# Staging the next layer's parameters and the sample state right behind the pooling, with a longer ring of input tiles, in a four-layer trunk

## The chip, the cores and the metric

The kernel runs on all 8 cores of one Trainium2 chip, each core with one prompt and 16 sample rows. The time is device microseconds of the slowest core. A program on 8 cores has a second, slower state in some executions, in which the cores of a die show a lower granted clock; fast runs are compared with fast runs here. Faster, same, slower are drawn at 2%. In the profiles PE is TensorE (the matrix engine, which also does the transposes), DVE is VectorE, ACT is ScalarE, POOL is the Pool engine (GpSimd) and SP is SyncE. A slab is one block of weights, a head one of the eight heads of the spatial step.

## The reference, cut to what matters

```python
for l in range(4):                       # for the prompt and for the sample rows
    z = rmsnorm(x, g_pre_mix) @ w_in      # columns a | u | v | gate_a | gate_b
    ya, new_buf = pool_mixer(a, buf, ...) # trailing means over 2..16 rows; the sample rows start from a state
    v = layernorm(gelu(v));  s = tril(W_s[h]) @ v + b_s[h]     # per head, chunks of 128 rows
    m = sigmoid(ga) * (ya @ w_ba) + sigmoid(gb) * ((gelu(u) * s) @ w_bb)
    x = x + rmsnorm(m @ w_out, ...)
    x = x + rmsnorm(relu(rmsnorm(x) @ w_up)**2 @ w_down, ...)
```

## The kernel before: the parts that matter

A core works through three blocks of rows (768, 768, and 512 plus the 128 sample rows), four layers each, in 128-row tiles: 6, 6 and 5 of them. The weights come as 30 slabs a layer (2 MB of f32 read, 1 MB of bf16 written) into 8 places.

A scheduler emits every instruction with the semaphore waits that its declared reads and writes need. A write waits for the last writer and for all readers of the name. Two things run through the Pool engine in one order: the issue of all slab loads and of the casting parameter loads, and the small steps of each norm, `(var + eps)` and `** -0.5`.

```python
def pool_dma(writes, out, in_, cost):
    key = ("g", nxt("g", 4))
    S.op("pool", [], writes, lambda e: e.dma_start(out=out, in_=in_), semkey=key, inc=16, ...)

def stage_params(l, par, ae):             # ae: the four names of the pooling buffer, which the parameters overlay
    pool_dma(["raw16"] + ae, raw16, w_spT[l]..., 1.5)
    pool_dma(["bb16"] + ae, bb16, ln_b[l:l + 1, :]..., 1.5)
    pool_dma(["wpg"], wpg[:, :, :], w_pg[l]..., 0.8)
    S.dma([], ["bsb"] + ae, bsb..., b_sp[l:l + 1, :]...)
```

The second load names `ae` too, so it waits until the first has landed.

The order of one layer, cut:

```python
head: clear or copy the first 15 columns of the pooling buffer; sample block: load the state, copy it in
for n in (0, 1):                          # two sub-blocks of tiles
    a_stage; start pooling (VectorE); u_stage; v_stage of each tile; start its LayerNorm chain
pool_proj(1)
for j in range(8):
    gate, branch A for j;  if j == 0: flush the LayerNorm chains;  spatial(j, 0); spatial(j, 1)
branch B, output projection, up-projection (first half)
CH.drain(); stage_params(next layer)      # no norm is in flight here
up-projection (second half), prep of the staged parameters between its slabs
down-projection; norm of each tile; start the next layer's norm, or store the tile and load the next block's
```

Of the kernel before, what the change touches and what calls it, by code (L numbers as in the profile page):

```python
# [170 lines left out]
def build():  # L171
# [35 lines left out]
    with es:  # L207
# [3 lines left out]
        def sb(name, shape, dt):  # L211
            return es.enter_context(nc.sbuf_tensor(name, shape, dt))

        x = sb("x", [128, 7, 1024], F32)
        hTb = sb("hTb", [128, 8 * TMAX], BF16)
        R2 = sb("R2", [128, 32 * TMAX], BF16)
        R1 = sb("R1", [128, 4 * AW], F32)
# [18 lines left out]
        invcnt = sb("invcnt", [128, 4, 15], F32)  # L236
        atail = sb("atail", [128, DEPTH, 4, 15], F32)
        t3 = [sb(f"t3_{i}", [128, 16], F32) for i in range(2)]
        spst = sb("spst", [128, 4, 16, 15], F32)
        stt = sb("stt", [128, 6, 8], F32)  # L240
        vstats = sb("vstats", [128, 6, 2, 6], F32)
        vmv = sb("vmv", [128, 6, 2], F32)
# [79 lines left out]
            return (b0[:, 0:512].bitcast(BF16).rearrange("p (h t) -> p h t", h=8), b0[:, 512:1024].bitcast(BF16),  # L322
                    b1.rearrange("p (h t) -> p h t", h=8))

        def stage_params(l, par, ae):
            raw16, bb16, bsb = par
            pool_dma(["raw16"] + ae, raw16, w_spT[l].rearrange("p (h t) -> p h t", h=8), 1.5)
            pool_dma(["bb16"] + ae, bb16, ln_b[l:l + 1, :].broadcast_to([128, 1024]), 1.5)
            pool_dma(["wpg"], wpg[:, :, :], w_pg[l].rearrange("p (g d) -> p g d", g=4), 0.8)
            S.dma([], ["bsb"] + ae, bsb.rearrange("p h t -> p (h t)"), b_sp[l:l + 1, :].broadcast_to([128, 1024]))  # L330

        def load_g(key, buf, src, l):
            S.dma([], [key], buf[:], src[l:l + 1, :].broadcast_to([128, 1024]))
# [40 lines left out]
        def group(parts, N, M=128):  # L374
            b = bank()
            total = sum(len(p[1]) for p in parts)
            at = 0
            for reads, mms in parts:
                pace()
                CH.pump()  # L380

                def emit(e, mms=mms, at=at):
                    for q, (lh, rh) in enumerate(mms):
                        r = e.matmul(ps[b][:, 0:N], lhsT=lh, rhs=rh, start=(at + q == 0), stop=(at + q == total - 1))  # L384
                    return r
                S.op("pe", reads, [("ps", b)], emit, cost=mm_us(len(mms), N))
                at += len(mms)
            CH.pump(False)
            return b

# [96 lines left out]
            return (BLOCKS[bi][1] + (128 if BLOCKS[bi][2] else 0)) // 128  # L487

        def xslot(bi, i):
            return (6 * bi + i) % 7  # L490

        def load_x(bi, i, after=[]):
            k = xslot(bi, i)
# [12 lines left out]
        for i in range(3):  # L506
            launch(i, lambda i=i: start_norm(i, xslot(0, i), views(768)["hT"]))
            need_hT([i])
            if i < 2:
                load_next()  # L510
        pool_dma(["trilT"], trilT[:], c_tril, 0.3)
        stage_params(0, par0, [])
        for i in range(3, 6):
            load_x(0, i, [("hT", i - 3)])
            launch(i, lambda i=i: start_norm(i, xslot(0, i), views(768)["hT"]))
# [6 lines left out]
        for bi, (p0, npr, samp) in enumerate(BLOCKS):  # L522
# [7 lines left out]
            if samp:  # L530
                gslot = xslot(bi, NT)
                gb32 = x[:, gslot, :]
                spare = R2[:, 32 * T:32 * T + 4096].bitcast(F32)
                bb32, vsamp = spare[:, 0:1024], spare[:, 1024:2048]

            for l in range(DEPTH):
# [3 lines left out]
                nsamp = has_next and BLOCKS[nbi][2]  # L540


                head = [("aext", g) for g in range(4)] + ["raw16", "bb16", "bsb"] + [("og0", i) for i in range(6)]
                if bi == 0:
                    S.op("dve", [], head,
                         lambda e: e.memset(aext[:, :, 0:15], 0.0), cost=0.15)
# [1 line left out]
                    S.op("dve", [("atail", l)], head,  # L548
                         lambda e: e.tensor_copy(out=aext[:, :, 0:15], in_=atail[:, l, :, :]), cost=0.15)
                if samp:  # L550
                    S.dma([], ["spst"], spst[:].rearrange("p g q r -> p (g q r)"), sp_in[l])
                    sx = aext[:, :, SBASE:SBASE + 368].rearrange("p g (q r) -> p g q r", r=23)
                    for g in range(4):
                        S.op("dve", ["spst"], [("aext", g)],
                             lambda e, g=g: e.tensor_copy(out=sx[:, g, :, 0:15], in_=spst[:, g, :, :]), cost=0.4)
                    R2tail = [] if l else [("fT", j, n) for j in range(32) for n in range(2)]
                    S.dma([], ["gb32", ("x", gslot)], gb32, ln_g[l:l + 1, :].broadcast_to([128, 1024]))
                    S.dma([], ["bb32"] + R2tail, bb32, ln_b[l:l + 1, :].broadcast_to([128, 1024]))
# [24 lines left out]
                def a_outputs():  # L583
                    ae = [("aext", g) for g in range(4)]
                    if bi < len(BLOCKS) - 1:
                        S.op("dve", ae, [("atail", l)],
                             lambda e: e.tensor_copy(out=atail[:, l, :, :], in_=aext[:, :, npr:npr + 15]), cost=0.15)
                    if samp:
                        S.op("dve", ae, ["atail_o"],
                             lambda e: e.tensor_copy(out=atail[:, l, :, :], in_=aext[:, :, npr:npr + 15]), cost=0.15)  # L590
                        S.dma(["atail_o"], [("spp", l)], spp[l], atail[:, l, :, :].rearrange("p g w -> p (g w)"))
                        for g in range(4):
                            S.op("dve", ae, ["spst"],
                                 lambda e, g=g: e.tensor_copy(out=spst[:, g, :, :], in_=sx[:, g, :, 8:23]), cost=0.4)
                        S.dma(["spst"], [("sps", l)], sps[l], spst[:].rearrange("p g q r -> p (g q r)"))

                def pool_chain(g, seg, ta, tb, tk, t3x, t3k):
                    kind, c0, L, n = seg
# [118 lines left out]

                for n, (n0, N) in enumerate(subs):
                    need_hT(stiles[n])
                    if n == 1:  # L720
                        load_g("gpre", gpre, g_pre_f, l)
                        load_g("gpost", gpost, g_pm, l)
                    a_stage(n, n0, N)
                    if n == 1:
                        a_outputs()
                        CH.flush(pooled)
                        release(bi, l, SL_A)
                    segs = []
                    pe_ = min(n0 + N, npr)
                    if pe_ > n0:  # L730
                        segs.append(("p", n0, pe_ - n0, n))
                    if samp and n == 1:
                        segs.append(("s", 0, 8, 1))
                    last_pooled = CH.start(pooling(segs))
                    u_stage(n, n0, N)
                    if n == 1:
                        pool_proj(0, *subs[0])
                    pooled = last_pooled
                    for i in stiles[n]:
                        v_stage(i)  # L740
                    if n == 0 and bi == 0 and l == 0:
                        for ph in range(3):
                            prep(samp, ph, par0)
                for q in (SL_U, SL_U + 1, SL_V, SL_V + 1):
                    release(bi, l, q)
                CH.flush(pooled)
                pool_proj(1, *subs[1])


                def gate(j, n, first, step):  # L750
# [50 lines left out]
                for j in range(8):  # L801
# [2 lines left out]
                        branch_a(j, n, q)  # L804
                    if j == 3:
                        release(bi, l, SL_GA)
                    if j == 0:
                        for c in ln:
                            CH.flush(c)
                    for n in range(2):  # L810
                        spatial(j, n)
                    if samp and j == 2:
                        S.op("dve", vk + ["gb32"], vk,
                             lambda e: e.tensor_tensor(out=vsamp, in0=vsamp, in1=gb32, op=ALU.mult), cost=1.2)
# [110 lines left out]
                load_g("gpost", gpost, g_pf, l)  # L925
                if last and has_next:
                    load_x(nbi, 0)
                if has_next:
                    stage_params(nl, parR, [("aext", g) for g in range(4)])
                    load_g("gpre", gpre, g_pre_m, nl)  # L930
                for s8 in range(4, 8):
                    for jj in range(4):
# [7 lines left out]
                for i in range(NT):  # L940
                    n = 0 if i < 3 else 1
                    parts = []
                    for q in range(4):
                        kw, sv = slab_kn(bi, l, SL_DN + q, 8)
                        parts.append(([kw] + [("fT", 8 * q + k, n) for k in range(8)],
                                      [(fT[:, 8 * q + k, i * 128:(i + 1) * 128], sv[:, k, :]) for k in range(8)]))
                    b = group(parts, 512)
                    if i == NT - 1:
                        for q in range(4):
                            release(bi, l, SL_DN + q)  # L950
                    jq = nxt("junk", 2)
                    S.op("act", [], [("ps", b), ("st", i, 0), ("junk", jq)],
                         lambda e: e.activation(out=junk[jq][:, 0:512], in_=ps[b][:, :], func=AF.Square, scale=1.0 / 32.0,  # L953
# [8 lines left out]
                def ffn_chain(i, b, q, bi=bi, last=last, has_next=has_next, nbi=nbi, nV=nV):  # L962
# [16 lines left out]
                    if not last:  # L979
                        launch(i, lambda: start_norm(i, xk, nV["hT"]))  # L980
                    else:
                        S.dma([("x", xk)], [("y", bi, i)], x_dst(bi, i), x[:, xk, :], lat=6.0)
                        if has_next and i + 1 < ntiles(nbi):
                            yield S.ready(("y", bi, i)), False
                            load_x(nbi, i + 1)
                            launch(i + 1, lambda: start_norm(i + 1, xslot(nbi, i + 1), nV["hT"]))

                if last and has_next:
                    launch(0, lambda: start_norm(0, xslot(nbi, 0), nV["hT"]))

                ffn = {}
                for i in range(NT):
                    n = 0 if i < 3 else 1
                    parts = []
                    for q in range(4):
                        kw, sv = slab_kn(bi, l, SL_DN + 4 + q, 8)
                        parts.append(([kw] + [("fT", 8 * q + k, n) for k in range(8)],
                                      [(fT[:, 8 * q + k, i * 128:(i + 1) * 128], sv[:, k, :]) for k in range(8)]))
                    b = group(parts, 512)
                    if i >= 2:  # L1000
                        CH.flush(ffn[i - 2])
                    ffn[i] = CH.start(ffn_chain(i, b, i % 2))
                for q in range(4):
                    release(bi, l, SL_DN + 4 + q)
                for i in range(NT):
                    CH.flush(ffn[i])
            if bi == len(BLOCKS) - 1:
# [94 lines left out]
```

## Time and profile before

| | before |
|---|---|
| fast runs | 3795.09, 3794.92 us (its other two, 3874.82 and 4460.84 us, were slow) |
| span of the 8 cores in the profiled run | 3772.0 to 3795.0 us |
| granted TensorE clock | 0.990 to 0.993 |
| TensorE busy | 3667.3 us, 97% |

A table of waits reads: engine, line and what it writes, then what ended the wait, then the total in us, the number of waits and the longest.

### The profile page before, as it was taken

Reading aid. Unit: us, or ns where it says so; the run is one execution under the profiler, and the core shown is the slowest. Engines: PE = TensorE matmul, PEld = TensorE weight load, DVE = VectorE, ACT = ScalarE, POOL = GpSimd, SP = SyncE. Lnnn points to the kernel's source line nnn. Section 1 sums busy time; section 2 is a strip of 40 time slices with the busy share of each in tenths; the row PEclk is TensorE's granted clock in tenths of the full one; section 3 lists DMA queues with packets and bytes.
Section 4 is the critical chain, followed back from the end, with each engine's and each line's share of the span. In section 5 each row is a group of like instructions: output and inputs, shape, how many; then the busy total and the mean of one; then the engine's idle time right before and its main releaser. Section 6 shows DMA issues by size and latency. Waiting matters only on the chain.

```text
span 3795.0 us, 63764 instructions; the slowest of 8 cores (3772.0 to 3795.0 us)
## 1 busy us (share of the span) xinstructions
PE 3667.3 (97%) x22021; PEld 2105.6 (55%) x22208; DVE 1764.7 (47%) x3385; ACT 1160.6 (31%) x2528; POOL 527.6 (14%) x1219
## 2 busy tenths in 40 slices
PE   6999999999999999999999999998899999999999
PEld 3554555555455455555545555553565665664664
DVE  3642652563455256246426525642552752752752
ACT  2331332323233133323313323241332331331331
POOL 1111110111101011011111101111011111111110
PEclk9999999999999999999999999999899999999999
DMA  8484766658467675755756666595677777777773
GB/s 165 81 149 76 124 107 103 112 98 147 78 112 117 116 152 96 135 98 92 127 97 112 103 111 111 92 157 125 130 119 143 137 124 143 137 124 141 140 121 86
DMA packets 75194, 449.32 MB, mean 118 GB/s; under 512 B 9472, under 2 KB 11136, under 8 KB 28800
## 3 DMA queue, kind: packets, MB, share of 16 engines
q0 software_dynamic: 57456, 385.48, 61.9%
q1 hardware_dynamic: 17424, 59.76, 5.1%
q8 instruction: 185, 3.03, 0.3%
q14 instruction: 129, 1.06, 0.1%
HBM read 817.55 MB, written 13.10 MB: 219 GB/s over the span
## 4 chain that ended last, share of the span: by engine, by line
PE 92%; DMA 5%; issue 1%; DVE 1%; ACT 0%; POOL 0%; DVEq 0%; SPq 0%; ACTq 0%; POOLq 0%
PE ps L384 84%; PE ps L883 6%; DMA R<-w_spT 2%; PE ps L439 2%; DMA R<-b_sp 1%; DMA R<-ln_b 1%; PE ps L778 1%; DMA x<-xp 1%; DMA spst<-sp 1%; ACT R L393 0%; DVE ps L837 0%; DVE hTb L445 0%; PE ps L364 0%; DVE x L976 0%; DVE R L685 0%
## 5 line engine op out<-in xcount | busy, mean ns | idle before, releaser
L384 PE MATMUL ps<-hTb,wslot 128*128 128x384 bf16 (+1 forms) x11520 | 1868.1, 319 | 18.3 <-DVE Cm L369 9.4
L384 PEld LDWEIGHTS ps<-hTb,wslot 128*128 128x128 bf16 x11520 | 1125.1, 98 | 668.9 <-issue 41.1
L384 PE MATMUL ps<-wslot,R 128*128 128x512 bf16 x4254 | 938.9, 379 | 5.3 <-issue 0.2
L393 ACT ACTIVATE R<-ps 128x384 bf16<-128x384 f32 (+5 forms) x1208 | 576.8, 482 | 958.7 <-PE ps L384 913.8
L384 PEld LDWEIGHTS ps<-wslot,R 128*128 128x128 bf16 x4352 | 424.5, 98 | 503.7 <-issue 0.2
L901 DVE TENSOR_TENSOR R<-R 128x384 bf16<-128x384 bf16 (+1 forms) x768 | 263.0, 346 | 558.6 <-ACT R L393 556.5
L384 PE MATMUL ps<-R,wslot 128*128 128x384 bf16 (+1 forms) x2304 | 414.1, 318 | 0.6
L306 POOL DMA_DIRECT2D wslot<-wslab x360 | 201.5, 563 | 971.5 <-PE ps L384 479.2
L393 ACT ACTIVATE sg<-ps 128x384 bf16<-128x384 f32 (+1 forms) x384 | 179.8, 471 | 495.9 <-PE ps L384 262.0
L384 PEld LDWEIGHTS ps<-R,wslot 128*128 128x128 bf16 x2304 | 225.2, 98 | 129.8 <-issue 3.4
L431 DVE SCALAR_TENSOR_TENSOR hst<-x,stt,gpre 128x1024 bf16<-128x1024 f32 x136 | 174.4, 1283 | 164.1 <-POOL stt L404 161.3
L956 DVE TENSOR_TENSOR R<-ps,gpost 128x512 f32<-128x512 f32 x68 | 47.1, 692 | 432.3 <-ACT junk L953 432.3
L883 PE MATMUL ps<-wslot,R 128*128 128x512 bf16 x1024 | 234.7, 379 | 3.4
L384 PE MATMUL ps<-wslot,hTb 128*128 128x512 bf16 x1063 | 233.7, 379 | 1.3
L422 ACT ACTIVATE hst<-x 128x1024 bf16<-128x1024 f32 x136 | 143.5, 1055 | 193.8 <-DVE x L976 122.5
L384 PEld LDWEIGHTS ps<-wslot,hTb 128*128 128x128 bf16 x1088 | 106.4, 98 | 125.6
L953 ACT ACTIVATE junk<-ps 128x512 bf16<-128x512 f32 x68 | 40.6, 597 | 427.1 <-PE ps L384 427.1
L883 PEld LDWEIGHTS ps<-wslot,R 128*128 128x128 bf16 x1088 | 105.6, 98 | 116.4
L404 POOL TENSOR_TENSOR stt<-stt,mhalf 128x1 f32<-128x1 f32 x272 | 163.4, 601 | 40.1 <-POOL stt L426 0.6
L837 DVE TENSOR_TENSOR ps<-ps,sg 128x384 f32<-128x384 f32 (+1 forms) x192 | 104.1, 542 | 128.5 <-PE ps L384 127.1
L854 ACT ACTIVATE junk<-ps 128x512 bf16<-128x512 f32 x136 | 81.2, 597 | 270.2 <-PE ps L883 247.1
L706 DVE BATCH_NORM_STATS2 vstats<-R 128x6 f32<-128x512 bf16 x128 | 88.9, 694 | 155.5 <-ACT R L393 155.5
(73 smaller groups left out, 1817.2 us busy)
## 6 DMA issues: line engine op xcount, KB each, us to landing
wslot<-wslab POOLq DMA_DIRECT2D x360, 1024.0 KB, 16.4
x<-xp SPq DMA_DIRECT2D x16, 512.0 KB, 6.9
yp<-x SPq DMA_DIRECT2D x16, 512.0 KB, 9.8
gpre<-g_pre_m SPq DMA_DIRECT2D x12, 512.0 KB, 21.1
R<-b_sp SPq DMA_DIRECT2D x12, 512.0 KB, 12.9
gpre<-g_pre_f SPq DMA_DIRECT2D x12, 512.0 KB, 15.0
gpost<-g_pm SPq DMA_DIRECT2D x12, 512.0 KB, 21.2
gpost<-g_pf SPq DMA_DIRECT2D x12, 512.0 KB, 5.1
```

The source lines that it names most:

```text
L306: lambda e: e.dma_start(out=wslot[k][:, :], in_=wslab[l, s]), semkey=("w", k), inc=16, cost=5.7, lat=2.0)
L384: r = e.matmul(ps[b][:, 0:N], lhsT=lh, rhs=rh, start=(at + q == 0), stop=(at + q == total - 1))
L393: lambda e: e.activation(out=out, in_=in_, func=func, **kw), cost=act_us(N))
L404: lambda e: e.tensor_tensor(out=col, in0=ss, in1=mhalf[:, 0:n], op=ALU.pow))
L422: lambda e: e.activation(out=hst[q][:, :], in_=x[:, k, :], func=AF.Square, scale=1.0 / 32.0, accum_out=stt[:, i, 4:5]), cost=1.2)
L431: lambda e: e.scalar_tensor_tensor(out=hst[q][:, :], in0=x[:, k, :], scalar=stt[:, i, 5:6], in1=gpre[:, :], op0=ALU.mult, op1=ALU.mult), c ...
L439: r = e.transpose(out=pT16[:, c * 128:(c + 1) * 128], in_=hst[q][:, c * 128:(c + 1) * 128], identity=ident16[:])
L706: lambda e: e.bn_stats(out=vstats[:, i, half, :], in_=B3[:, i, cs]), cost=0.69)
L837: lambda e: e.tensor_tensor(out=ps[b][:, 0:N], in0=ps[b][:, 0:N], in1=sgring[q][:, 0:N], op=ALU.mult), cost=dve_us(N))
L854: lambda e, b=b, ci=ci: e.activation(out=junk[jq][:, 0:512], in_=ps[b][:, :], func=AF.Square, scale=1.0 / 32.0, accum_out=stt[:, i, ci:ci ...
L883: r = e.matmul(ps[b][:, :], lhsT=B2[:, k, i * 128:(i + 1) * 128], rhs=wo[:, k, :], start=(k == 0), stop=(k == 7))
L901: lambda e: e.tensor_tensor(out=fT[:, j, n0:n0 + N], in0=fT[:, j, n0:n0 + N], in1=fT[:, j, n0:n0 + N], op=ALU.mult), cost=dve_us(N, 2))
```

## The change

Its intent: take the waits at the block boundaries, at the layer ends of the sample block and at the start out of TensorE's way. Cut to its core (lines left out or gathered; where the source has an edit in several places it stands once):

```diff
-        x = sb("x", [128, 7, 1024], F32)
+        x = sb("x", [128, 8, 1024], F32)          # the state now lies in a free place of this ring
 # start
-            if i < 2:
-                load_next()                        # slabs 2, 3 between the first norms
+        load_next(); load_next()                   # after the third norm
-        stage_params(0, par0, [])
+        stage_params(0, par0, [], [("hT", 0)])     # b_sp waits for the first norm
 # head of a layer
-    head = [...aext...] + ["raw16", "bb16", "bsb"] + [...]
+    head = [...aext...] + [...];  if bi or l: head += ["raw16", "bb16", "bsb"]
-    S.dma([], ["spst"], ..., sp_in[l]);  copy spst into aext      # sample block
+    if l == 0: S.dma([], ["spst", ("x", sslot)], ..., sp_in[l])
 # sub-block n == 1
+    if n == 1 and samp: copy spst into aext
 # behind the pooling
     CH.flush(pooled)
     pool_proj(1, *subs[1])
+    if has_next:
+        stage_params(nl, parR, [("aext", g) for g in range(4)])
+    if samp and not last:
+        S.dma([], ["spst"], ..., sp_in[l + 1])
 # gates
-    if j == 0: flush the LayerNorm chains
-    for n in range(2): spatial(j, n)
+    if j == 1: flush the LayerNorm chains
+    for h in ((), (0,), (1,), (2,), (3,), (4, 5), (6,), (7,))[j]:
+        for n in range(2): spatial(h, n)
 # up-projection
-    stage_params(nl, parR, [("aext", g) for g in range(4)])
 # down-projection: each slab is released after its own part of the last tile, not all four at the end
 # next block: tiles 0 and 1 loaded ahead, tile i + 2 (not i + 1) after the store of tile i
```

More of the change, by code (lines that the diff above doesn't have):

```diff
@@ L238, in build @@
         t3 = [sb(f"t3_{i}", [128, 16], F32) for i in range(2)]
-        spst = sb("spst", [128, 4, 16, 15], F32)
         stt = sb("stt", [128, 6, 8], F32)
@@ L323, in par_views_of, with stage_params @@
                     b1.rearrange("p (h t) -> p h t", h=8))
-        def stage_params(l, par, ae):
+        def stage_params(l, par, ae, after=[]):
             raw16, bb16, bsb = par
@@ L329, in stage_params @@
             pool_dma(["wpg"], wpg[:, :, :], w_pg[l].rearrange("p (g d) -> p g d", g=4), 0.8)
-            S.dma([], ["bsb"] + ae, bsb.rearrange("p h t -> p (h t)"), b_sp[l:l + 1, :].broadcast_to([128, 1024]))
+            S.dma(after, ["bsb"] + ae, bsb.rearrange("p h t -> p (h t)"), b_sp[l:l + 1, :].broadcast_to([128, 1024]))
         def load_g(key, buf, src, l):
@@ L377, in group @@
             at = 0
-            for reads, mms in parts:
+            for part in parts:
+                reads, mms = part[:2]
                 pace()
@@ L387, in group @@
                 at += len(mms)
+                if len(part) > 2:
+                    part[2]()
             CH.pump(False)
@@ L489, in xslot @@
         def xslot(bi, i):
-            return (6 * bi + i) % 7
+            return (6 * bi + i) % 8
         def load_x(bi, i, after=[]):
@@ L508, in build @@
             need_hT([i])
-            if i < 2:
-                load_next()
+        load_next()
+        load_next()
         pool_dma(["trilT"], trilT[:], c_tril, 0.3)
-        stage_params(0, par0, [])
+        stage_params(0, par0, [], [("hT", 0)])
         for i in range(3, 6):
@@ L532, in build @@
                 gb32 = x[:, gslot, :]
+                sslot = xslot(bi, NT + 1)
+                spst = x[:, sslot, 0:960].rearrange("p (g q r) -> p g q r", g=4, q=16)
                 spare = R2[:, 32 * T:32 * T + 4096].bitcast(F32)
@@ L540, in build @@
                 nsamp = has_next and BLOCKS[nbi][2]
-                head = [("aext", g) for g in range(4)] + ["raw16", "bb16", "bsb"] + [("og0", i) for i in range(6)]
+                head = [("aext", g) for g in range(4)] + [("og0", i) for i in range(6)]
+                if bi or l:
+                    head += ["raw16", "bb16", "bsb"]
                 if bi == 0:
@@ L550, in build @@
                 if samp:
-                    S.dma([], ["spst"], spst[:].rearrange("p g q r -> p (g q r)"), sp_in[l])
+                    if l == 0:
+                        S.dma([], ["spst", ("x", sslot)], spst.rearrange("p g q r -> p (g q r)"), sp_in[l])
                     sx = aext[:, :, SBASE:SBASE + 368].rearrange("p g (q r) -> p g q r", r=23)
-                    for g in range(4):
-                        S.op("dve", ["spst"], [("aext", g)],
-                             lambda e, g=g: e.tensor_copy(out=sx[:, g, :, 0:15], in_=spst[:, g, :, :]), cost=0.4)
                     R2tail = [] if l else [("fT", j, n) for j in range(32) for n in range(2)]
@@ L594, in a_outputs @@
                                  lambda e, g=g: e.tensor_copy(out=spst[:, g, :, :], in_=sx[:, g, :, 8:23]), cost=0.4)
-                        S.dma(["spst"], [("sps", l)], sps[l], spst[:].rearrange("p g q r -> p (g q r)"))
+                        S.dma(["spst"], [("sps", l)], sps[l], spst.rearrange("p g q r -> p (g q r)"))
                 def pool_chain(g, seg, ta, tb, tk, t3x, t3k):
@@ L719, in build @@
                     need_hT(stiles[n])
+                    if n == 1 and samp:
+                        for g in range(4):
+                            S.op("dve", ["spst"], [("aext", g)],
+                                 lambda e, g=g: e.tensor_copy(out=sx[:, g, :, 0:15], in_=spst[:, g, :, :]), cost=0.4)
                     if n == 1:
@@ L747, in build @@
                 pool_proj(1, *subs[1])
+                if has_next:
+                    stage_params(nl, parR, [("aext", g) for g in range(4)])
+                if samp and not last:
+                    S.dma([], ["spst"], spst.rearrange("p g q r -> p (g q r)"), sp_in[l + 1])
                 def gate(j, n, first, step):
@@ L806, in build @@
                         release(bi, l, SL_GA)
-                    if j == 0:
+                    if j == 1:
                         for c in ln:
                             CH.flush(c)
-                    for n in range(2):
-                        spatial(j, n)
+                    for h in ((), (0,), (1,), (2,), (3,), (4, 5), (6,), (7,))[j]:
+                        for n in range(2):
+                            spatial(h, n)
                     if samp and j == 2:
@@ L927, in build @@
                     load_x(nbi, 0)
+                    load_x(nbi, 1)
                 if has_next:
-                    stage_params(nl, parR, [("aext", g) for g in range(4)])
                     load_g("gpre", gpre, g_pre_m, nl)
@@ L945, in build @@
                         parts.append(([kw] + [("fT", 8 * q + k, n) for k in range(8)],
-                                      [(fT[:, 8 * q + k, i * 128:(i + 1) * 128], sv[:, k, :]) for k in range(8)]))
+                                      [(fT[:, 8 * q + k, i * 128:(i + 1) * 128], sv[:, k, :]) for k in range(8)],
+                                      lambda q=q, i=i: i == NT - 1 and release(bi, l, SL_DN + q)))
                     b = group(parts, 512)
-                    if i == NT - 1:
-                        for q in range(4):
-                            release(bi, l, SL_DN + q)
                     jq = nxt("junk", 2)
@@ L982, in ffn_chain @@
                         S.dma([("x", xk)], [("y", bi, i)], x_dst(bi, i), x[:, xk, :], lat=6.0)
-                        if has_next and i + 1 < ntiles(nbi):
+                        if has_next and i + 2 < ntiles(nbi):
                             yield S.ready(("y", bi, i)), False
-                            load_x(nbi, i + 1)
-                            launch(i + 1, lambda: start_norm(i + 1, xslot(nbi, i + 1), nV["hT"]))
+                            load_x(nbi, i + 2)
+                            launch(i + 2, lambda: start_norm(i + 2, xslot(nbi, i + 2), nV["hT"]))
                 if last and has_next:
-                    launch(0, lambda: start_norm(0, xslot(nbi, 0), nV["hT"]))
+                    for i in range(2):
+                        launch(i, lambda i=i: start_norm(i, xslot(nbi, i), nV["hT"]))
                 ffn = {}
@@ L997, in build @@
                         parts.append(([kw] + [("fT", 8 * q + k, n) for k in range(8)],
-                                      [(fT[:, 8 * q + k, i * 128:(i + 1) * 128], sv[:, k, :]) for k in range(8)]))
+                                      [(fT[:, 8 * q + k, i * 128:(i + 1) * 128], sv[:, k, :]) for k in range(8)],
+                                      lambda q=q, i=i: i == NT - 1 and release(bi, l, SL_DN + 4 + q)))
                     b = group(parts, 512)
@@ L1002, in build @@
                     ffn[i] = CH.start(ffn_chain(i, b, i % 2))
-                for q in range(4):
-                    release(bi, l, SL_DN + 4 + q)
                 for i in range(NT):
```

## The prediction

> **What bounds the kernel now.** I read the cores first (3772.0 to 3795.0 us, granted clock 0.990 to 0.993 on every core, the state is fast), then the engines, the matmul engine's waits over the whole span and by stretch, and then the order of time around each wait. The page says that TensorE is the bound:
>
> ```profile
> PE 3667.3 (97%) x22021; PEld 2105.6 (55%) x22208; DVE 1764.7 (47%) x3385; ACT 1160.6 (31%) x2528; POOL 527.6 (14%) x1219
> ```
>
> 3795.0 - 3667.3 = 127.7 us is all that a change of order can win. The change adds no matmul and removes none. The waits of PE (us in total, times, longest) say where those us are:
>
> ```profile
> PE ps L439 <- DVE hst L431: 60.3, 8, 26.9
> PE ps L778 <- DVE R L685: 11.8, 8, 2.2
> PE ps L384 <- DVE Cm L369: 9.4, 3, 4.2
> PE ps L384 <- DVE R L642: 9.2, 4, 2.3
> PE ps L348 <- DVE WmT L339: 6.7, 3, 2.9
> PE ps L384 <- ACT R L393: 4.2, 1, 4.2
> ```
>
> Asked by stretch, row 1 is 27.8 us at the start, 5.5 at the first block boundary (1341 us) and 26.9 at the second (2644 us). Row 2 is one wait in each of the 8 layers of the first two blocks: the first spatial matmul waits for LayerNorm of the last tile. Rows 3 and 5 are three layer ends of the sample block, waiting for the next layer's spatial parameters. The 26.9 us are plain in the order of VectorE and then TensorE:
>
> ```profile
> 2647.51 0.19 DVE L549 COPY R<-atail 128x60 f32<-128x60 f32 x1
> 2668.22 0.86 DVE L555 COPY R<-spst 128x240 f32<-128x240 f32 x4 [20.51 <-DMA spst<-sp]
> ...
> 2671.02 1.01 PE L439 MATMUL ps<-ident,hst 128*128 128x128 bf16 x8 [26.86 <-DVE hst L431]
> 2672.97 5.13 PE L384 MATMUL ps<-hTb,wslot 128*128 128x384 bf16 x16 [0.94 <-DVE hTb L445]
> ```
>
> VectorE runs in order; the copies of the sample state stand ahead of the norms of the new tiles and wait 20.5 us for their transfer.
>
> The view that decides my prediction is the Pool queue, which carries weight slabs, staged parameters and the little square roots of every norm. First, today's staging, in the middle of a layer's up-projection:
>
> ```profile
> 564.69 0.53 POOL L306 DMA_DIRECT2D wslot<-wslab  x1 [4.67 <-PE ps L384]
> 565.47 0.53 POOL L278 DMA_DIRECT2D R<-w_spT  x1 [0.25 <-issue]
> 581.54 0.53 POOL L278 DMA_DIRECT2D R<-ln_b  x1 [15.55 <-DMA R<-w_spT]
> 582.09 0.53 POOL L278 DMA_DIRECT2D wpg<-w_pg  x1
> ```
>
> Pool stands still 15.55 us between the first staged load and the second. The cause is in the code: all staged loads declare that they write the pooling buffer as a whole, so the second waits until the first has landed. Over the run this is 187.4 us in 11 waits. Today it costs PE nothing, since at that place no norm is in flight. Now the place to which the change moves it, Pool and then PE:
>
> ```profile
> 425.91 1.69 POOL L306 DMA_DIRECT2D wslot<-wslab  x3
> 428.45 0.22 POOL L669 TENSOR_SCALAR vrs<-vmv 128x1 f32<-128x1 f32 x1 [0.85 <-DVE vmv L708]
> 428.82 0.57 POOL L404 TENSOR_TENSOR vrs<-vrs,mhalf 128x1 f32<-128x1 f32 x1
> ...
> 426.21 0.81 PE L384 MATMUL ps<-R,wpg 128*128 128x384 bf16 x4
> 426.86 1.46 PE L384 MATMUL ps<-hTb,wslot 128*128 128x384 bf16 x8
> ...
> 432.46 0.33 PE L778 MATMUL ps<-WmT,R 128*128 128x128 bf16 x3 [1.37 <-DVE R L685]
> ...
> 436.52 0.50 PE L778 MATMUL ps<-WmT,R 128*128 128x128 bf16 x6
> ```
>
> The four wpg matmuls are the last pooling projection. After them the changed code stages the parameters. The three slab loads are emitted during the projection, and the last tile's LayerNorm steps (vrs) after it: their variance comes only at 428.3. I printed the emission order of the kernel before while it is built, and it says the same in all 8 layers of blocks one and two. In the sample block the last tile's vrs comes before that place.
>
> **The Trainium skill.** "DMA: Bandwidth & Descriptors", Queues, rings and completion order: an engine takes a ring's descriptors in ring order and round-robins between rows. The trace agrees: the three slabs issued at 425.91, 426.53 and 427.05 landed 10.9, 16.7 and 23.1 us later, some 6.5 us apart; and the w_spT load above landed 1.25 us after the slab ahead of it, 15.5 us after its issue, though it is only 256 KB. The same page, Two DMAs through the same engine are not ordered, tells the author to let the issuing engine wait on the first transfer's semaphore; that is what Pool does in the 15.55 us. "TensorE: Matmul & The Clock Gate", What's actually happening: after an idle window of about 3.4 us the array restarts at half clock for about as long. The trace agrees: the 16 matmuls after the 26.86 us took 5.13 us, 0.32 us each; in an undisturbed stretch 8 take 1.46 us.
>
> **The change, part by part.**
>
> 1. *Sample state copied before the second sub-block, loaded a layer ahead; x ring of 8 with two tiles prefetched.* At the second boundary VectorE no longer stands behind the state, and tile 2 can be loaded after tile 0's store instead of tile 1's. Waits at the boundaries now: 5.5 + 0.9 and 26.9 + 0.9 = 34.2 us. With the two half-clock restarts (24 matmuls 6.11 us instead of 3.9; 16 in 5.13 instead of 2.6; twice 0.4 us in transposes) about 39 us. I keep 1 us: -38.
> 2. *Staging early, seen from the sample block.* Its three waits for parameters, 9.4 + 6.7 = 16.1 us, vanish, with some 1 us of slow restart each: -19. In this block the norm is ahead of the staging on Pool, so nothing is lost; slab loads come some 15 us later, but slabs stand ready long before use.
> 3. *Staging early, seen from the 8 layers of blocks one and two.* Call the end of the last wpg matmul E. The third slab lands at E+22.2 to E+23.8 in these layers (from the trace, mean 23.0). w_spT lands 1.3 us behind it: E+24.3. Then Pool issues ln_b (0.53 to start, 0.55), wpg (0.55), and does the tile's two vrs steps (0.94); 0.1 to the next engine, and VectorE normalises (0.95, as 431.51 to 432.46): 3.6 us. The tile is ready at E+27.9. PE meanwhile goes through two gate steps (3.9 us each, 426.9 to 430.76 and 432.62 to 436.52) and the first half of head 0, and is in need of the tile at E+7.9. The delay of the spatial matmuls by one step, made for the old wait of 1.5 us, covers 3.9 us. New wait: 20.0 us a layer, 160 in 8 layers. Each is long enough for a half-clock restart, 2.5 us as at the second boundary: +20. The old L778 waits, 11.8 us, are contained in it: -12.
> 4. *First loads.* Tile 2 landed at 24.17 us while sharing with slabs; without the second and third slab ahead, perhaps 2 us sooner, and the 4.2 us wait behind ACT goes, as the buffer's clearing no longer waits for ln_b (46.85 us). But the V projection then waits for its second slab, which lands at 61.2 us after a transfer backlog that has the same bytes in it. I count -2.
> 5. *Slabs released part by part.* The first of four slabs is asked for up to 3 x 1.7 = 5 us sooner. No wait of PE on a slab is in the list: 0.
>
> Sum: -38 - 19 + 160 + 20 - 12 - 2 = +109. 3795 + 109 = 3904; I say 3905 us.
>
> **Rivals.** *The gains stand alone* (the staged load lands soon, or the norm's Pool steps slip ahead of it): 3795 - 38 - 19 - 12 - 2, about 3724 us, 1.9% faster. For it speaks that the author delayed head 0 by a step and so looked at this very place; against it, that the wait between staged loads stood in all 11 layers, and that three slabs are ahead in the ring. *The wait is half as long* (the loads are issued later than the slabs' start suggests, or slabs move faster when nothing is queued behind them): 10 us a layer instead of 20, about 3825 us, 0.8% slower, "same". Against it: the third slab's landing varies by only 1.6 us over the layers. *The delay spreads*: with Pool held for 25 us, the slabs of the output projection are asked for at E+28 instead of E+2.5 and stop PE again. They are needed some 35 us after the gates begin plus 21 us of branch B, later than E+28 plus 10 us to land; I add nothing, but it draws the range upward.
>
> **Range and chances.** Steps 1 and 2 are sure to some 10 us, step 4 to 6, step 3 to 30 if its order is right, which I believe at nine in ten. A fast run then lies between 3850 and 3960. Over 2% slower begins at 3871: 0.86. Within 2%: 0.10. Faster by over 2% needs more than every gain I see: 0.04.
>
> **What would show it.** PE's waits should list spatial matmuls (the line of L778) waiting 8 times for some 20 us each on the LayerNorm of the last tile, in blocks one and two alone; the Pool queue there should read slabs x3, w_spT, a wait of 24 us, ln_b, wpg, vrs. The boundaries' waits and those on Cm and WmT should be gone. I am wrong if Pool shows the vrs steps ahead of w_spT, or the wait on w_spT is under 10 us at that place, or PE finds the tile ready.

## The result, and the profile after

A ratio is the mean time of one kernel's fast runs over that of the other's fast runs of the same rounds, so not quite the ratio of the medians or single times quoted.

| | before | after |
|---|---|---|
| fast runs, us | 3795.09, 3794.92 | 3904.31, 3904.12 |
| ratio | 1 | 1.0288 (95%: 1.0244 to 1.0332) |
| slowest core, profiled run | 3795.0 | 3903.1 |
| TensorE busy, us | 3667.3 | 3678.0 |

Slower. (Two further runs of after, 4159 and 4140 us, were slow and are left out.) First the engines' line and the waits of TensorE in the changed kernel; L790 is the spatial matmul that was L778, and L441 the transpose that was L439:

```profile
PE 3678.0 (94%) x22019; PEld 2108.3 (54%) x22208; DVE 1768.8 (45%) x3385; ACT 1160.9 (30%) x2528; POOL 542.9 (14%) x1219
```

```profile
PE ps L790 <- DVE R L689: 143.0, 8, 19.3
PE ps L441 <- DVE hst L433: 21.7, 3, 11.2
PE ps L384 <- DVE R L646: 12.5, 4, 3.1
PE ps L384 <- DMA wslot<-wslab: 9.9, 4, 5.6
PE ps L441 <- ACT R L395: 6.0, 9, 0.7
PE ps L384 <- DVE R L810: 4.9, 8, 0.9
...
PE ps L384 <- DVE hTb L447: 3.0, 2, 2.7
```

The waits that the change aimed at are gone: the transposes wait only at the start (21.7 us; the two boundary waits are missing), and no row names the staged parameters of a layer end. In their place stands one row of 143.0 us, 8 waits of 17.9 us on average on LayerNorm's last step (L689). By stretch, all 8 are in the first two blocks. Now the Pool queue at that place in the second layer, then TensorE:

```profile
444.93 1.69 POOL L305 DMA_DIRECT2D wslot<-wslab  x3
446.59 0.56 POOL L277 DMA_DIRECT2D R<-w_spT  x1
469.16 0.54 POOL L277 DMA_DIRECT2D R<-ln_b  x1 [22.01 <-DMA R<-w_spT]
469.77 0.53 POOL L277 DMA_DIRECT2D wpg<-w_pg  x1
470.38 0.22 POOL L673 TENSOR_SCALAR vrs<-vmv 128x1 f32<-128x1 f32 x1
470.75 0.57 POOL L406 TENSOR_TENSOR vrs<-vrs,mhalf 128x1 f32<-128x1 f32 x1
```

```profile
453.67 0.33 PE L790 MATMUL ps<-WmT,R 128*128 128x128 bf16 x3
472.45 0.48 PE L790 MATMUL ps<-WmT,R 128*128 128x128 bf16 x3 [18.45 <-DVE R L689]
472.72 2.76 PE L384 MATMUL ps<-hTb,wslot 128*128 128x384 bf16 x8
...
476.16 1.46 PE L384 MATMUL ps<-hTb,wslot 128*128 128x384 bf16 x8
```

Two steps of under 1 us together (vrs) stand behind a transfer that they have nothing to do with. Pool waits 22.01 us for w_spT before it may issue ln_b; the variance that vrs needs was there at 447.3 us. TensorE stands 18.45 us, and its first 8 matmuls then take 2.76 us instead of 1.46: the half clock that the prediction cites from the Trainium skill, "TensorE: Matmul & The Clock Gate", What's actually happening. The granted clock shows it too: 0.50 from 458.7 to 475.7 us, then 1.00.

The page of waits also closes the account. All listed waits of PE: 110 us before, 208 after, +98. Busy time, which includes the half-clock restarts: +10.7. Together +108, and the spans differ by 108.1. By the granted clock of the two traces TensorE worked 39.2 us at half clock before and 59.9 us after; half of the difference is 10.4 us, nearly all that the busy time grew by.

### The profile page after: what moved, and what is told of

It reads as the page before. It is cut to its first block, busy times and chain, and to the rows that moved or that the text cites. A ratio compares the mean times of both kernels' runs of the same rounds, so it can differ in the third digit from the quotient of the medians.

```text
span 3903.1 us, 63731 instructions; the slowest of 8 cores (3884.4 to 3903.1 us)
## 1 busy us (share of the span) xinstructions
PE 3678.0 (94%) x22019; PEld 2108.3 (54%) x22208; DVE 1768.8 (45%) x3385; ACT 1160.9 (30%) x2528; POOL 542.9 (14%) x1219
## 4 chain that ended last, share of the span: by engine, by line
PE 88%; DMA 6%; issue 2%; DVE 2%; ACT 1%; POOL 1%; DVEq 0%; POOLq 0%; ACTq 0%; SPq 0%
PE ps L384 80%; PE ps L896 6%; DMA R<-w_spT 4%; PE ps L441 1%; PE ps L790 1%; ACT R L395 1%; DMA trilT<-c_tril 0%; DMA x<-xp 0%; DMA wslot<-wslab 0%; DVE x L987 0%; POOL stt L411 0%; DVE ps L798 0%; ACT hst L424 0%; POOL wslot L305 0%; ACT junk L977 0%
## 5 line engine op out<-in xcount | busy, mean ns | idle before, releaser
L384 PE MATMUL ps<-hTb,wslot 128*128 128x384 bf16 (+1 forms) x11520 | 1871.5, 320 | 12.9 <-DMA wslot<-wslab 4.1
L384 PEld LDWEIGHTS ps<-R,wslot 128*128 128x128 bf16 x2304 | 226.3, 99 | 134.8 <-issue 11.1
L790 PE MATMUL ps<-WmT,R 128*128 128x128 bf16 x512 | 46.0, 223 | 145.2 <-DVE R L689 143.0
## 6 DMA issues: line engine op xcount, KB each, us to landing
gpre<-g_pre_m SPq DMA_DIRECT2D x12, 512.0 KB, 12.9
```

The costliest lines, as they stand in the source:

```text
L384: r = e.matmul(ps[b][:, 0:N], lhsT=lh, rhs=rh, start=(at + q == 0), stop=(at + q == total - 1))
L790: r = e.matmul(ps[b][:, ti * 128:(ti + 1) * 128], lhsT=B3[:, i, h * 128:(h + 1) * 128], rhs=Wt[:, h, :], start=True, stop=True)
```

## The experiments

**1. Remove the mutual wait.** If the theory is right, one declared dependency is the whole loss. The kernel is the changed one; each staged load still waits for every earlier reader and writer of the pooling buffer, but no longer for its fellow:

```diff
 def stage_params(l, par, ae, after=[]):
-    pool_dma(["raw16"] + ae, raw16, ...)
-    pool_dma(["bb16"] + ae, bb16, ...)
-    S.dma(after, ["bsb"] + ae, bsb..., ...)
+    old = [S.lw[k] for k in ae if k in S.lw] + [t for k in ae for t in S.rd.get(k, {}).items()]
+    pool_dma(["raw16"], raw16, ..., also=old)
+    pool_dma(["bb16"], bb16, ..., also=old)
+    S.dma(after, ["bsb"], bsb..., ..., also=old)
```

> The changed kernel, with one thing other: the staged loads wait for the readers of the pooling buffer, but no longer for one another. Theory (Pool stands still for w_spT's landing and holds back the last tile's two vrs steps): Pool issues w_spT, ln_b, wpg back to back within 2 us, the 8 spatial waits (143 us in the changed kernel) fall under 5 us in all, and with the half-clock restarts gone (8 x 2.5 us) the time is 3903 - 143 - 20 = 3740 us, 0.985 of the kernel before. Rival A (the transfers themselves are late: more bytes in the ring at that place): the waits stay above 10 us each, the time above 3870. Rival B (moving head 0 and the flush of the norms by a step is the cause): the waits stay too.

Measured: 3750.0 us, median of the three fast runs (a fourth, 3804.48 us, was slow), ratio 0.9865 (0.9849 to 0.9882). Pool in the second layer:

```profile
425.21 1.69 POOL L305 DMA_DIRECT2D wslot<-wslab  x3
426.87 0.56 POOL L277 DMA_DIRECT2D R<-w_spT  x1
427.39 0.57 POOL L277 DMA_DIRECT2D R<-ln_b  x1
427.97 0.53 POOL L277 DMA_DIRECT2D wpg<-w_pg  x1
428.57 0.22 POOL L674 TENSOR_SCALAR vrs<-vmv 128x1 f32<-128x1 f32 x1
```

The 8 waits are gone from the list altogether. By the trace w_spT still landed 22.8 us after its issue, so the transfers are as late as before, and rival A falls: it is not the lateness that costs, but that Pool waits for it. Rival B falls too, since head 0 and the flush are where the change put them. The wait protected nothing: w_spT and ln_b write different parts of the buffer, and the results stayed correct without it. 10 us of the forecast are missing: the eight restarts had cost 15 us and not 20 (see the last sections), and these rounds were slower (3801.6 us for the kernel before, not 3795).

**2. Only the staging put back.** The changed kernel with `stage_params` in the up-projection again:

```diff
 pool_proj(1, *subs[1])
-if has_next: stage_params(nl, parR, ...)
 ...
 if has_next:
+    stage_params(nl, parR, ...)
     load_g("gpre", gpre, g_pre_m, nl)
```

> The changed kernel with the staging of the parameters put back into the up-projection, all else as changed. Theory: the 8 spatial waits go, the three waits of the sample block (16 us, 19 with slow restarts) come back: 3740 + 19 = 3759 us, 0.990 of the kernel before. Rival B (the moved head and flush): the spatial waits stay and the time is about 3900.

Measured: fast runs 3773.23 and 3775.69 us, ratio 0.9929 (0.9909 to 0.9949). The spatial waits on LayerNorm are gone, and in the waits of PE the old rows are back:

```profile
PE ps L384 <- DVE Cm L368: 13.1, 3, 5.6
...
PE ps L347 <- DVE WmT L338: 5.7, 3, 2.5
```

The waits are as expected; the time is above the 3759 us said (ratio 0.993 for 0.990). Against experiment 1 these 18.8 us of waits cost some 24 us of time, half-clock work behind them included: that is what early staging is worth when nothing stands behind it.

**3. Only the staging moved.** The kernel before, with nothing but `stage_params` behind the pooling; head 0 keeps its place in the first gate step.

> The kernel before with only the staging moved behind the pooling; head 0 keeps its place. Theory: the tile is ready some 25.8 us after the last wpg matmul as in the changed kernel, but PE needs it one gate step (3.9 us) earlier, so each of the 8 waits is 21.8 us, 174 in all against 11.8: 3795 + 162 + 20 (restarts) - 19 (sample block) = 3958 us, 1.043 of the kernel before, slower than the whole change. Rival B: no slower than the kernel before.

Measured: 3949.2 us median, ratio 1.0389 (1.0374 to 1.0404).

```profile
PE ps L780 <- DVE R L685: 181.7, 8, 24.1
```

22.7 us a wait, where 21.8 was forecast and the whole change has 17.9. So the bad part alone loses more than the whole change, and the one-step delay of head 0 does what it was made for: the waits differ by 4.8 us, where one gate step takes 3.9. But that is 4.8 us of some 22.

**4. w_spT ahead of the slabs.** This asks what sets the length of the wait. The mutual wait stays; w_spT is only issued before the last pooling projection, during which the three slabs are emitted:

```diff
 CH.flush(pooled)
+if has_next: stage_first(nl, parR, ...)      # w_spT
 pool_proj(1, *subs[1])
-if has_next: stage_params(nl, parR, ...)
+if has_next: stage_rest(nl, parR, ...)       # ln_b, wpg, b_sp
```

> The changed kernel with w_spT issued before the last pooling projection, so ahead of the three slabs in the ring; ln_b still waits until it has landed. Theory (the length of the wait is the three slabs of 6.5 us in front): w_spT lands in 4 to 7 us instead of 22, Pool is free some 17 us sooner, the spatial waits fall from 17.9 to 0 to 3 us each, the time is 3740 to 3775 us, 0.985 to 0.995 of the kernel before. Rival C (the wait is a fixed cost of a staged load, slabs or not): it stays above 12 us each and the time above 3850.

Measured: 3754.6 us, median of the fast runs, ratio 0.9875 (0.9858 to 0.9891). Pool, second layer:

```profile
433.21 0.62 POOL L277 DMA_DIRECT2D R<-w_spT  x1
433.83 1.07 POOL L305 DMA_DIRECT2D wslot<-wslab  x2
438.94 0.53 POOL L277 DMA_DIRECT2D R<-ln_b  x1 [4.04 <-DMA R<-w_spT]
```

4.04 us instead of 22.01, and w_spT landed 5.2 us after its issue instead of 22.0. The same load, the same wait in the code; what made it long was the three slabs issued ahead of it. Rival C falls. The LayerNorm wait of TensorE is gone from the list.

**5. The sample state alone**, on the kernel before: the copies go before the second sub-block, the load a layer ahead, in its own buffer.

> The kernel before with one part alone: the sample state's copies stand before the second sub-block, and its load comes a layer ahead (its own buffer, x ring of 7). Theory (the 26.9 us at the second boundary are VectorE behind those copies): the wait of the transposes there falls to about that of the first boundary, 5.5 us; the pooling waits of the sample block rise from 2.3 to 3.1 us each (0.86 us of copies now stand right before the pooling): 3800 - 21 + 3 = 3782 us, 0.995. Rival (the tile's own load is late there, since the ring has 7 places): the wait stays above 15 us, no gain.

Measured: ratio 0.9952 (0.9932 to 0.9971), 3785.5 us, median of the fast runs. At the second boundary, and over the span:

```profile
PE ps L439 <- DVE hst L431: 5.5, 1, 5.5
```

```profile
PE ps L384 <- DVE R L640: 12.4, 4, 3.1
```

26.9 became 5.5 us, equal to the first boundary. The pooling waits rose from 9.2 to 12.4 us in all, for the copies now stand right before the pooling. Both as expected; what is left for the longer ring, which was not run alone, is two waits of 5.5 us with their restarts.

**6. The start alone**, on the kernel before (the slabs after the third norm, b_sp after the first, the buffer's clearing freed of the parameters).

> The kernel before with the start alone changed: second and third slab after the third norm, b_sp after the first norm, the buffer's clearing no longer behind the parameters. My step: the V projection's second slab still lands near 60 us, so waits only change their names (transposes and ACT out, slab transfers in), 0 to -2 us, 0.9995 to 1.0. Rival (the first projection starts 4 us sooner and keeps that lead): 0.998 or less.

Measured: ratio 1.0003 (0.9978 to 1.0027). In the first 100 us the transposes wait 23.0 us (27.8 before), the 4.2 us behind ACT are gone, and this is new:

```profile
PE ps L384 <- DMA wslot<-wslab: 11.8, 4, 5.4
```

The waits changed their names, as step 4 said.

**7. The release by parts alone**, on the kernel before.

> The kernel before with the slabs of the down-projection released part by part, alone. PE waits for no slab in the kernel before, so the theory is no change within 2 us, ratio 0.9995 to 1.0005; the first of the four slabs is issued some 5 us sooner in the trace. Rival (slabs are late at the head of a layer): 5 us a layer at most, 0.985.

Measured: ratio 1.0019 (0.9984 to 1.0054): no gain, and the interval is too wide to call 2 us (its four fast runs spread from 3799.5 to 3824.7 us, and the profile is of the slowest of them, with a lower clock on some cores of die 1; what follows is from core 0, clock 0.993). By the trace the first of the four slabs is issued 4.9 us before the end of the first layer's down-projection, where the kernel before issues it 2.2 us after, so 7 us sooner where I expected 5. On Pool it now stands ahead of norm steps of the last tiles: at 361.5 us the slab's issue ended a wait of 3.58 us for TensorE, and the next norm step came at 362.1 us, right behind it. The profile lists six waits of transposes for ScalarE, 3.8 us in all, that the kernel before does not list. What the part is worth alone can't be told from this run.

**8. Head 0 in its old place in the sample block**, on the kernel of experiment 1. There the norm was never late.

```diff
-if j == 1:
+if j == (0 if samp else 1):
     for c in ln: CH.flush(c)
-for h in ((), (0,), (1,), (2,), (3,), (4, 5), (6,), (7,))[j]:
+for h in ((j,) if samp else ((), (0,), (1,), (2,), (3,), (4, 5), (6,), (7,))[j]):
```

> The kernel with the mutual waits removed, and head 0 in its old place in the sample block, where the norm was never late. The two waits of branch B and of the spatial matmuls on the products of the heads (4.9 + 2.2 us there, absent in the kernel before) should vanish: 3750 - 7 = 3743 us, 0.985 of the kernel before. Rival (these waits have another cause, such as VectorE being full): they stay.

Of its four runs one was fast, 3738.78 us, so there is no ratio. It was run again with five rounds:

> The parent of the run beside it once more, since its first three rounds fell almost all in the slow state: 3740 us, 0.984 of the kernel before.

Measured: ratio 0.9839 (0.9825 to 0.9854), fast runs 3735.96 to 3741.35 us. The waits on the heads' products fell from 7.1 to 0.3 us. The interval just overlaps that of experiment 1, so the gain is read from these waits more than from the times. The delay of head 0, made to hide one wait, had cost another where that wait did not exist.

**9. An attempt at a better one**: the kernel of experiment 8 with the slabs of the down-projection released together again, and the state copied at the head from the second layer on.

> The kernel with mutual waits removed and head 0 in its old place in the sample block; in addition the slabs of the down-projection are released together again (a slab load that waits for PE stood ahead of the last tile's norm steps on Pool: nine waits of transposes, 0.7 us each, 5.9 in all), and the state is copied at the layer's head from the second layer on, where it has long landed (3 x 0.8 us of pooling wait). Theory: 8 us less than its parent: 3731 us, 0.982 of the kernel before. Rival (early release is worth its place in the changed kernel): no faster than the parent.

Measured: ratio 0.9842 (0.9829 to 0.9855), 3740.09 us median, no faster than its parent beside it. The nine transposes' waits did go, and the pooling waits fell to 10.1 us, but at each of the two block boundaries its waits of PE have these rows, which the parent does not have at all:

```profile
PE ps L385 <- DVE hTb L448: 4.3, 1, 4.3
PE ps L442 <- DVE hst L434: 1.0, 1, 1.0
```

By the trace, at the first boundary the first four of the next block's slabs are issued some 5.6 us later, counted from the end of the down-projection (41.9 us before it at 1339.4 us, in the parent 47.4 us before it at 1333.3 us), so more of them shares the queues with the tiles' stores and loads: the second store took 12.8 us, in the parent 7.4, the load of tile 2 took 11.2 us, in the parent 5.2, and each next tile waits for a store. Of the two edits only the release can act at the first boundary, as the other stands in the sample block; that the shared queues are how it acts is argued, not tried apart. So in this kernel the release by parts saves about 10 us of waits at the boundaries (twice 4.3 + 1.0); whether it needs the longer ring for that was not tried. Experiments 8 and 9 are the fastest versions found and equal within the noise. Experiment 8 is 1.6% below the kernel before, which by the 2% rule is "same", and 4.4% below the changed one (0.9839 / 1.0288 = 0.956).

## Why the prediction was right

The time was 3904 us where 3905 was said. The mechanism is the one that was predicted; that the total fits to 1 us is luck, as terms that were wrong by 22 us cancel. The measured terms are waits from the lists and, for the restarts, half of TensorE's busy time in the stretches at half clock (matmuls take nearly twice as long there, so half of it is lost):

- **Step 1, boundaries, -38 us.** 34.2 us of waits fell to 2.7 (near the first boundary) and 0, and 11.1 us of work at half clock, 5.5 us lost, went with them: -37. Right; experiment 5 gave the state's share.
- **Step 2, sample block, -19 us.** The waits went, 16.1 us, and 12.9 us of half-clock work behind them: -22.5. Experiment 2 against 1 makes it some 24 us.
- **Step 3, the new wait, +168 us (160 + 20 - 12).** The mechanism is shown by experiments 1, 3 and 4, each of which moves one of its links. Its size was 143.0 us, not 160. Taking the second layer, with E the end of its last wpg matmul at 446.0 us: w_spT landed at 468.6 us, E+22.6 instead of E+24.3 (over the eight layers E+22.0 on average). The fourth slab, which followed at once in the kernel before, is now itself held back; in experiment 1, where it follows again, w_spT landed at E+23.5 on average, so that slab can account for some 1.5 of the 2.3 us, and the rest is open. The way from there to the spatial matmul took 3.8 us (3.6 said), and PE was in need at E+8.0 (7.9 said). The restarts were too dear as well: the rows after 472.45 us lost 0.15 + 1.30 + 0.23 = 1.7 us, and the eight together 15 us (29.9 us of work at half clock; 1.3 to 3.0 us each), where 2.5 each was said. That figure came from the second boundary, where the clock stayed at half for 6.8 us after the wait. 143 + 15 - 12 = 146 us.
- **Step 4, start, -2 us.** Nothing (experiment 6).
- **Step 5, releases, 0 us.** Not quite. In the changed kernel they cost nine waits of up to 0.7 us: a slab load that waits for TensorE now stands on Pool ahead of the last tile's norm steps, the same mistake in small. And they save about 10 us at the boundaries (experiment 9), which is part of step 1.
- **What the sum left out:** the pooling waits of the sample block, 9.2 us before and 12.5 after (+3.3 us). Each grew only from 2.3 to 3.1 us, but in these two profiles all four of the longer ones were followed by half clock and only two of the shorter: 18.4 us of work at half clock instead of 6.8, so +5.8 us more. Then these transposes (+6.0) and the heads' products (4.9 + 2.2). Together 22 us, as much as step 3 had too many.

-37 - 22.5 + 146 + 22 = 108.5 us, where the spans differ by 108.1.

None of the rivals held. "The gains stand alone" is what experiment 1 shows once the link is cut: 3750 us. Of the 26 us to the 3724 said, some 22 are the terms that the sum left out, and these rounds were also some 6 us slower.

## What to carry to other kernels

Before moving a wait to a place where it "costs nothing", list what stands behind it on the same in-order queue there, not only what its own result is needed for. An engine that issues transfers and also computes small steps of a chain should not be made to wait for a landing while such a chain is in flight (here it cost 143 us); and a dependency declared on a whole buffer by several loads is such a wait. How long it lasts is set by what is queued ahead of the transfer, here three slabs (3 MB written), not by the transfer's own 256 KB: 22.0 us behind them, 5.2 us ahead of them (experiment 4).

## What the Trainium skill lacked or had wrong

- "DMA: Bandwidth & Descriptors", Anatomy of one DMA, says that any semaphore wait happens on the issuing sequencer. It does not draw the consequence for Pool, which also computes: two steps of 0.79 us together were held behind a wait of 22.01 us. No page that I read warns of this.
- The same page, Bandwidth, has 1 MB at 6.15 us for one core alone, without a word on a transfer that casts. Here slabs that read 2 MB of f32 and write 1 MB of bf16, on 8 cores at once, landed some 6.5 us apart (kernel before, second layer).
- "TensorE: Matmul & The Clock Gate", What's actually happening: about 3.4 us at half clock, so an estimate of 1.7 us lost, fits the eight restarts (1.3 to 3.0 us, 1.9 on average) better than the 2.5 us that I took from the boundary. So the page was not wrong there; but its length is not a fixed one here: at the boundary half clock lasted 6.8 us after the wait, which "for about as long" in the prediction passes over.
